# A trunk kernel's first microseconds: the first weights fetched earlier, one half's square sum put after the other half's scaling

## The chip, the core and the metric

The kernel runs on one core of one Trainium2 chip. The metric is the device time of one execution in microseconds (us). The core has a matrix engine (PE; its weight loads are listed as PEld), a vector engine (DVE), a scalar engine (ACT), a general engine (POOL) and a queue engine that only issues transfers (SP). Each engine takes its instructions in the order in which the program lists them.

## What is computed

Two layers of a causal decoder trunk over 256 tokens of width 1024, in float32:

```python
for i in range(DEPTH):                        # DEPTH = 2
    hn = rms_norm(x, norm_mix[i])
    mix = even_mixer(hn, ...) if i % 2 == 0 else odd_mixer(hn, ...)
    x = x + mix
    x = x + sqrelu_mlp(rms_norm(x, norm_mlp[i]), mlp_w1[i], mlp_w2[i])
return rms_norm(x, norm_final)
# rms_norm: y = xf * rsqrt(mean(xf * xf, axis=-1) + EPS) * g
```

What matters here is the very first step, `rms_norm(x, norm_mix[0])`, and the first product with the layer's weights.

## The kernel before

**Tiling.** x is held as two tiles of 128 tokens, `X[0]` and `X[1]` (the first and the second half). A half is normed, transposed by PE in blocks of 128x128 against an identity matrix, and stored as a high and a low part (`xTh`, `xTl`), since each float32 product is made of three products of shortened numbers. Weights come as 196 pieces of up to 128x1024 (512 KB); `raw` is a piece as fetched, `whi` and `wlo` are its two parts, written by ACT (line 470, called "high split" here) and DVE (line 473, "low split"). Pieces 0, 1 and 2 (840, 840 and 560 columns) are the weights of the first unit, `vg`: 280 output columns, eight k steps for each half of x, three matmuls a k step. Pieces 0, 1 and 2 carry k steps 0-2, 3-5 and 6-7. Pieces 3 and 4 are the next unit, `k`. Five raw buffers exist, so five pieces may be fetched before the first is split.

**The start.** Line 501 loads `X[0]`, line 502 the norm weight `gB`, line 503 the identity, line 504 starts the generator `loads()` (lines 447 to 454), which asks for one piece after the other, line 505 loads `X[1]`, lines 506 and 507 two tables (`cst`, `prm`). All are issued on SP. In `first_norms` (lines 894 to 919) PE first spreads `gB` over all rows (line 899); then for each half `rstd` (line 534) takes the square sum, half of the columns on ACT (line 543) and half on DVE (line 546), POOL adds them and takes the power -1/2 (lines 555 and 557), DVE scales two blocks of 512 columns (line 911), PE transposes each block (line 593), ACT writes `xTh` (line 515) and DVE writes `xTl` (line 521).

**Who sets the order.** The program's order is not written out by hand. A planner (`Plan`, lines 201 to 313) plays a rough model of the engines while the program is being written: each step has an assumed duration and an urgency (lower goes first), and an engine that falls free takes the most urgent step whose inputs are there in the model. The order in which steps begin in the model is the order of the instructions on the chip; the chip then keeps to it, whatever arrives first in fact. A step sees another engine's result 0.2 us later (`SEEN`), and a generator that waits for another line's event or for a buffer is held up by 0.2 us as well. A transfer lands, in the model, at the time that line 406 gives:

```python
Plan.moved = max(Plan.moved, plan.now + lat) + n / 0.34e6   # lat 1.3 us, n in bytes
plan.at(Plan.moved + 0.5, lambda: plan.fire(ev))
```

The steps of the norm have urgency -4 (first half) and -3 (second half), the splits of the pieces that are needed next -1, most others 0 to 3. After the unit `vg` the planner places the set-up of a bias table (`bias_setup`, a table look-up by PE at line 709), then the unit `k` with its matmuls at lines 530 to 532.

Of the kernel before, what the change touches and what calls it, by code (L numbers as in the profile page):

```python
# [25 lines left out]
PSUM = bass.MemoryType.PSUM  # L26
# [174 lines left out]
class Plan:  # L201
    """Puts the program's steps out in the order in which a rough model of the engines begins them:
    each engine takes the most urgent step whose inputs are there."""
# [17 lines left out]
    def when(self, deps, line, fn):  # L221
        """Calls fn as soon as the line can see all of deps done."""
        deps = [d for d in deps if d is not None]
        left = [sum(d.time is None for d in deps)]

        def go():
            t = max([self.now] + [d.time + (0.0 if d.line in (line, None) else SEEN) for d in deps])
            self.at(t, fn)

        def one():  # L230
            left[0] -= 1
            if not left[0]:
                go()

        if not left[0]:
            go()
        else:
            for d in deps:
                if d.time is None:
                    d.then.append(one)  # L240

    def step(self, choices, deps=(), urgency=1, bank=None):
        """choices: (line, time, emit) of the engines that can do the step."""
        self.count += 1
        s = Step(urgency, self.count, bank)
        for line, dur, emit in choices:
            self.when(deps, line, lambda line=line, dur=dur, emit=emit: self.arrive(line, s, dur, emit))
        return s.done
# [44 lines left out]
    def spawn(self, gen):  # L293
        """Runs gen; each value it yields is the events it waits for."""
        ev = Event()

        def go():
            try:
                w = next(gen)
            except StopIteration:  # L300
                self.fire(ev)
                return
            w = [w] if isinstance(w, Event) else w
            self.when(w, None, go)

        self.at(self.now, go)
        return ev
# [8 lines left out]
class Slots:  # L316
    """Buffers that are handed on; the one who gets it waits for its last use."""
# [22 lines left out]
    def recall(self, item):  # L340
        """Takes an item out as soon as it is free."""
        ev = Event()
        if any(item is i for i in self.items):
            self.items = [i for i in self.items if i is not item]
            self.plan.fire(ev)
        else:
            self.wanted.append((item, ev))
        return ev
# [14 lines left out]
@with_exitstack  # L363
def trunk_kernel(ctx: ExitStack, tc: tile.TileContext, x, w, prm_d, gs, cst_d, eye, out, widths):
# [7 lines left out]
    plan = Plan()  # L372
# [24 lines left out]
    def load(dst, src, deps=(), line=SP, u=0, lat=1.3):  # L397
        """A transfer: issued by an engine, then in turn with the others on the queues."""
        eng = {SP: nc.sync, ACT: nc.scalar, POOL: nc.gpsimd}[line]
        n = int(np.prod(dst.shape)) * 4  # L400
        ev = Event()
        dur = {SP: 0.45, ACT: 0.4, POOL: 1.04}[line]
        issued = plan.step([(line, dur, lambda: eng.dma_start(dst, src))], deps, u)

        def move():
            Plan.moved = max(Plan.moved, plan.now + lat) + n / 0.34e6
            plan.at(Plan.moved + 0.5, lambda: plan.fire(ev))

        plan.when([issued], None, move)
        return ev  # L410
# [4 lines left out]
    def halves(pair):  # L415
        """Room for two pieces in a pair of tiles that are not in use."""
        v = [a.rearrange("p k s -> p (k s)") for a in pair]
        return [(v[0][:, 1024 * i:1024 * i + 1024], v[1][:, 1024 * i:1024 * i + 1024]) for i in range(2)]
# [28 lines left out]
    def loads():  # L447
        for p, n in enumerate(widths):
            got = raws.get()
            yield got  # L450
            r = got.value[:, :n]
            src = bass.AP(tensor=w.tensor, offset=w.offset + int(starts[p]), ap=[[n, 128], [1, n]])
            ev = load(r, src, [got], u=1)
            plan.when([ev], None, lambda p=p, raw=got.value: plan.fire(loaded[p], SP, raw))
# [48 lines left out]
    ident_e = load(ident, eye)  # L503
    plan.spawn(loads())
    x_e.append(load(X[1], x[128:256, :], u=0.5))
# [5 lines left out]
    def split_out(hi, lo, src, n, deps, scale=None, bank=None, u=0):  # L511
        """The high part by ACT, the rest by DVE."""
        def high():
            if scale is None:
                nc.scalar.activation(hi, src, AF.Copy)
            else:
                nc.scalar.activation(hi, src, AF.Copy, scale=scale)

        def low():
            if scale is None:  # L520
                nc.vector.tensor_tensor(lo, src, hi.bitcast(F32), OP.subtract)
            else:
                nc.vector.scalar_tensor_tensor(lo, src, scale, hi.bitcast(F32), op0=OP.mult, op1=OP.subtract)  # L523

        e = act(t_act(n), high, *deps, u=u, bank=bank)
        return [e, dve(t_dve(n), low, e, u=u, bank=bank)]
# [7 lines left out]
    def rstd(t, deps):  # L534
        """(mean(x[t]^2) + eps)^-1/2; ACT squares the left columns and DVE the right ones, starting from the left's
        sum where those come first."""
# [22 lines left out]
    def rvar(t, deps):  # L559
        """1 / (mean(x[t]^2) + eps)."""  # L560
# [6 lines left out]
    def to_xT(t, g, xT, xe, rs, deps, back=()):  # L567
        """Steps that write x[t] * g (* rs) transposed into xT."""
# [78 lines left out]
    def unit_N(src, cuts, n, done):  # L647
        """One bank of columns for each row tile."""
        pcs = [next_piece() for _ in cuts]
        for t in range(2):  # L650
            got = bank_a.get()
            yield got
            prev = got
            for pc, (k0, nk) in zip(pcs, cuts):
                prev = rows_N(src, got.value, t, pc, k0, nk, n, prev)
                if t:
                    pc.release(prev)
            plan.spawn(done(t, got.value, [prev]))
# [3 lines left out]
    def units_N(src, dones):  # L662
        """Two banks of columns for each row tile; part of the second comes before the second tile's first."""
# [16 lines left out]
    def row_mm(bank, src, deps, pc, kt, t, n, prev, first, last, u=1):  # L680
        """bank += rows t of src's column tile kt @ half n of the piece's columns."""
# [57 lines left out]
    begun = []  # L739

    def urgency():
        """Earlier maps go first."""
# [3 lines left out]
    def logits_exp(q, k, par, h, P, sums, b, deps, u):  # L746
        """exp(q.k + bias - max) of one map: [q0 x k0 | q1 x k0 k1], and the row sums."""
# [30 lines left out]
    def turned_P(A, deps, u):  # L778
        """The transposed probabilities, in two parts."""
# [24 lines left out]
    def head_map(q, k, par, h, v, v_e, gate, pair, deps, seen=None):  # L804
        """One causal softmax map of a head; its part of the pair's outputs is added to po."""
# [32 lines left out]
    class Pair:  # L838
        """The outputs of two heads, gathered in one bank."""
# [27 lines left out]
    # ================= layer 0: mixer =================  # L867
# [26 lines left out]
    def first_norms():  # L894
        """g over all rows by the tensor engine; it stays in PSUM for the time."""
# [5 lines left out]

        def first_norm(t):
            rs, e = rstd(t, [x_e[t]])
            yield e
            done = []
            for hf in range(2):
# [6 lines left out]
                plan.spawn(turn_x(t, hf, xT0[0], xT0[1], xs, done[-1], ()))  # L913
            if t == 1:
# [11 lines left out]
    def got_ckv(b, evs):  # L926
        """Both parts of the compression's inputs, the second half-block's tokens below the first's."""
# [14 lines left out]
    def stack_q(dst, ps, b, deps, u=0):  # L942
        """Both parts of q / 8 of a head's rows: one in the head's half, the other in the other half."""
# [11 lines left out]
    def stack_k(hi, lo, ps, b, deps, u=0):  # L955
        """The high part of k twice, and the low part over zeros."""
# [92 lines left out]
    def cmp_hidden(ba, e):  # L1049
        """Compressed keys and values."""  # L1050
# [51 lines left out]
    def cmp_softmax():  # L1102
        """The compressed branch of the eight heads in one."""
# [176 lines left out]
    def add_to_x(bank, slots, dep, t, n, rs=None):  # L1280
        """x[t] += bank (* rs)."""
# [11 lines left out]
    def out_proj(m_e, x_free, nxt):  # L1293
        """x += m @ w; the first tokens go ahead, and their norm runs beside the products of the others.
        Two of the pieces lie in the room of the transposed x."""
# [38 lines left out]
    def mlp(src, x_ready, nxt):  # L1334
        """x += relu(norm(x) @ w1)^2 @ w2, the norm's factor of each token squared at the end."""
# [21 lines left out]
        def turned(t, b, evs):  # L1357
            """Tokens are the rows here: to be turned."""
# [76 lines left out]
    def next_stage(gi, norm):  # L1435
        """The transposed (normed) x of the next stage, one token tile after the other."""
# [19 lines left out]
    def program():  # L1456
# [19 lines left out]
        # layer 1  # L1476
# [44 lines left out]
    def final(t, evs):  # L1521
# [4 lines left out]
        def job():  # L1526
            """x * g waits for the norm's factor."""
# [40 lines left out]
```

## Time and profile before

| | |
|---|---|
| median of 3 runs | 640.43 us (640.12 to 640.68) |
| span of the profiled execution | 638.6 us |
| PE busy | 623.5 us (98% of the span) |
| DVE busy | 402.3 us (63%) |
| ACT busy | 358.8 us (56%) |
| clock granted to PE over the span | 0.996 of full |

The span is counted from the first to the last instruction of the profiled execution; the 1.8 us between it and the median lie around it. The profile has a page with totals and 40 slices of the span, and views that can be asked for a stretch: the timeline (instructions by engine in order of time), the table of waits, the transfers with their time to landing, and a table of busy times by stretch. A PE that is busy 98% of the span leaves little: what matters is where the other 2% lie, and in what order things happen around them.

### The profile page before, as it was taken

How to read it: one execution, taken by the hardware profiler on the slowest of the kernel's cores; microseconds unless marked ns; L12 is line 12 of the kernel's file. 1: busy time of each engine (PE TensorE's matmuls, PEld its weight loads, DVE VectorE, ACT ScalarE, POOL GpSimd, SP SyncE). 2: the span in 40 equal slices, each digit the busy share in tenths (PEclk: the TensorE clock that was granted, in tenths of full speed). 3: DMA queues.
4: the chain of work that ended last, by engine and by line, in shares of the span. 5: the costliest groups of instructions: out<-in, count | busy, mean ns of one | idle time of the engine just before them, and what ended most of it. 6: DMA issues, size and time to landing. Idle time of an engine off the chain costs nothing.

```text
span 638.6 us, 10541 instructions
## 1 busy us (share of the span) xinstructions
PE 623.5 (98%) x4022; PEld 562.5 (88%) x4022; DVE 402.3 (63%) x723; ACT 358.8 (56%) x645; POOL 80.8 (13%) x105
## 2 busy tenths in 40 slices
PE   7999999999999999999999999999999999999995
PEld 5999899778899898999988999978889999898994
DVE  6888698869554545445477688785964454544434
ACT  6777488747645445444444588764764444445421
POOL 2022022210201001011120020110020100101011
PEclk8999999999999999999999999999999999999999
DMA  7995432325765565656527433443576555565501
GB/s 280 320 304 190 141 105 96 131 101 185 256 212 191 179 199 165 204 191 214 183 73 236 155 121 111 132 133 120 173 267 202 195 179 193 176 200 176 165 2 66
DMA packets 33188, 110.49 MB, mean 173 GB/s; under 512 B 3425, under 2 KB 6769, under 8 KB 33138
## 3 DMA queue, kind: packets, MB, share of 16 engines
q1 hardware_dynamic: 32274, 107.21, 51.7%
q0 software_dynamic: 576, 2.10, 0.9%
q8 instruction: 31, 0.51, 0.3%
q10 hardware_dynamic: 288, 0.52, 0.2%
q14 instruction: 19, 0.16, 0.1%
HBM read 107.76 MB, written 1.07 MB: 170 GB/s over the span
## 4 chain that ended last, share of the span: by engine, by line
PE 86%; DVE 6%; ACT 4%; issue 2%; DMA 1%; POOL 1%; SPq 0%; POOLq 0%; DVEq 0%; ACTq 0%
PE ps L531 26%; PE ps L530 26%; PE ps L532 26%; PE ps L756 2%; DVE wlo L473 2%; PE ps L790 1%; DVE KZ L964 1%; PE ps L593 1%; DVE QD L951 1%; ACT KD L961 1%; DMA x<-in_x_dram 1%; ACT QD L947 1%; POOL P L827 1%; ACT KD L960 1%; PE ps L1040 1%
## 5 line engine op out<-in xcount | busy, mean ns | idle before, releaser
L473 DVE TENSOR_TENSOR wlo<-raw,whi 128x1024 fp32r<-128x1024 f32 (+1 forms) x157 | 189.3, 1217 | 74.1 <-ACT whi L470 72.6
L470 ACT ACTIVATE whi<-raw 128x1024 fp32r<-128x1024 f32 (+1 forms) x157 | 163.5, 1052 | 96.8 <-PE ps L532 70.3
L530 PE MATMUL ps<-xTh,whi 128*128 128x256 f32 x592 | 168.9, 285 | 0.0
L531 PE MATMUL ps<-xTl,whi 128*128 128x256 f32 x592 | 166.4, 281 | 0.0
L532 PE MATMUL ps<-xTh,wlo 128*128 128x256 f32 x592 | 166.3, 281 | 0.0
L530 PEld LDWEIGHTS ps<-xTh,whi 128*128 128x128 f32 x592 | 111.7, 189 | 1.1 <-ACT gates L996 0.3
L531 PEld LDWEIGHTS ps<-xTl,whi 128*128 128x128 f32 x592 | 111.7, 189 | 0.7
L532 PEld LDWEIGHTS ps<-xTh,wlo 128*128 128x128 f32 x592 | 111.6, 189 | 0.0
L1348 POOL TENSOR_TENSOR P<-P 128x512 f32<-128x512 f32 x32 | 35.8, 1120 | 320.5 <-ACT P L1345 319.0
L473 DVE TENSOR_TENSOR mTl<-raw,mTh 128x1024 fp32r<-128x1024 f32 x34 | 43.2, 1272 | 23.9 <-ACT mTh L470 23.9
L470 ACT ACTIVATE mTh<-raw 128x1024 fp32r<-128x1024 f32 x34 | 36.0, 1059 | 30.2 <-PE ps L531 20.4
L1345 ACT ACTIVATE P<-ps 128x512 f32<-128x512 f32 x32 | 19.0, 595 | 52.2 <-PE ps L532 52.2
L530 PE MATMUL ps<-whi,Th 128*128 128x512 f32 x120 | 46.9, 391 | 0.0
L532 PE MATMUL ps<-whi,Tl 128*128 128x512 f32 x120 | 46.9, 391 | 0.0
L531 PE MATMUL ps<-wlo,Th 128*128 128x512 f32 x120 | 46.9, 390 | 0.0
L1350 DVE TENSOR_TENSOR Tl<-P,Th 128x512 fp32r<-128x512 f32 x22 | 15.2, 693 | 50.1 <-POOL P L1348 50.1
L770 ACT ACTIVATE P<-P,nm 128x128 f32<-128x128 f32 x80 | 35.5, 447 | 13.5 <-DVE nm L766 13.5
L532 PE MATMUL ps<-xTh,mTl 128*128 128x256 f32 (+1 forms) x128 | 38.1, 297 | 0.7 <-DVE mTl L523 0.7
L530 PE MATMUL ps<-xTh,mTh 128*128 128x256 f32 (+1 forms) x128 | 38.7, 302 | 0.0
L531 PE MATMUL ps<-xTl,mTh 128*128 128x256 f32 (+1 forms) x128 | 38.0, 297 | 0.0
L530 PE MATMUL ps<-whi,xTh 128*128 128x512 f32 (+1 forms) x88 | 34.2, 389 | 0.0
L531 PE MATMUL ps<-wlo,xTh 128*128 128x512 f32 (+1 forms) x88 | 33.3, 378 | 0.2 <-DVE wlo L473 0.2
(219 smaller groups left out, 1193.0 us busy)
## 6 DMA issues: line engine op xcount, KB each, us to landing
raw<-in_w_dram SPq DMA_DIRECT2D x192, 512.0 KB, 4.1
B<-ud SPq DMA_DIRECT2D x1, 2048.0 KB, 11.3
gB<-in_gs_dram POOLq DMA_DIRECT2D x4, 512.0 KB, 4.3
x<-in_x_dram SPq DMA_DIRECT2D x2, 512.0 KB, 4.4
mTl<-kcv SPq DMA_DIRECT2D x4, 240.0 KB, 6.8
raw<-in_w_dram SPq DMA_DIRECT2D x2, 420.0 KB, 6.2
out_dram<-P SPq DMA_DIRECT2D x2, 256.0 KB, 2.0
out_dram<-P ACTq DMA_DIRECT2D x2, 256.0 KB, 2.5
```

The costliest lines, as they stand in the source:

```text
L470: nc.scalar.activation(pc.hi[:, :n], raw[:, :n], AF.Copy)
L473: nc.vector.tensor_tensor(pc.lo[:, :n], raw[:, :n], pc.hi[:, :n].bitcast(F32), OP.subtract)
L530: nc.tensor.matmul(out_, ah, bh, start=start, stop=False)
L531: nc.tensor.matmul(out_, ah, bl, start=False, stop=False)
L532: nc.tensor.matmul(out_, al, bh, start=False, stop=stop)
L593: nc.tensor.transpose(p[:, 128 * k:128 * k + 128], xs[:, 128 * k:128 * k + 128], ident)
L756: nc.tensor.matmul(ps[:, 128 * qt:128 * qt + nk], q[:, par, ts], k[i][:, par, :nk], start=i == 0, stop=i == 1)
L770: nc.scalar.activation(P[:, c], P[:, c], AF.Exp, bias=nm[:, qt:qt + 1], scale=-1.0, accum_out=sums[:, qt:qt + 1])
L790: nc.tensor.transpose(pt[:, c], A[:, c], ident)
L1345: e = act(t_act(512), lambda: nc.scalar.activation(r, b.t, AF.Relu), got, *deps)
L1348: g = pool(1.225, lambda: nc.gpsimd.tensor_tensor(sq, r, r, OP.mult), e)
L1350: h = dve(t_dve(512), lambda: nc.vector.tensor_tensor(hl, sq, hh.bitcast(F32), OP.subtract), f, g)
```

## The change

Three things are changed in the code. The first piece's load gets urgency 0.2 and `loads()` is started ahead of the identity's load, whose urgency becomes 0.4; with `X[1]`'s 0.5 unchanged, SP's order goes from `X[0]`, `gB`, identity, `X[1]`, piece 0, piece 1, ... to `X[0]`, `gB`, piece 0, identity, `X[1]`, piece 1, .... And the second half's norm now begins (both its square sums on ACT and DVE) only when an event `scaled` has fired, which stands for the first half's second scaling; before, it could begin as soon as `X[1]` had landed in the model. The rest of the diff takes out comments.

```diff
-            ev = load(r, src, [got], u=1)
+            ev = load(r, src, [got], u=0.2 if p == 0 else 1)
...
     x_e = [load(X[0], x[0:128, :])]
     g_e = load(gB[0:1, :], gs[0:1, :])
-    ident_e = load(ident, eye)
     plan.spawn(loads())
+    ident_e = load(ident, eye, u=0.4)
     x_e.append(load(X[1], x[128:256, :], u=0.5))
...
+        scaled = Event()
+
         def first_norm(t):
+            if t:
+                yield scaled
             rs, e = rstd(t, [x_e[t]])
             yield e
...
                 plan.spawn(turn_x(t, hf, xT0[0], xT0[1], xs, done[-1], ()))
+            if t == 0:
+                plan.when([done[-1]], None, lambda: plan.fire(scaled, DVE))
             if t == 1:
```

## Rows read from the trace of the kernel before

**Rows 1.** The page: span, PE's busy time, granted clock in 40 slices

```profile
span 638.6 us, 10541 instructions
PE 623.5 (98%) x4022; PEld 562.5 (88%) x4022; DVE 402.3 (63%) x723; ACT 358.8 (56%) x645; POOL 80.8 (13%) x105
PEclk8999999999999999999999999999999999999999
```

**Rows 2.** Waits over the span: who waited for whom, us, times, longest

```profile
PE ps L593 <- DVE P L911: 2.3, 1, 2.3
PE ps L530 <- DVE KZ L964: 1.8, 2, 1.1
PE ps L532 <- DVE mTl L523: 0.7, 1, 0.7
```

**Rows 3.** Timeline, PE and POOL: start, duration, what, idle before and releaser

```profile
4.30 2.25 PE L899 MATMUL ps<-gB,P 1*128 1x512 f32 x4
5.33 0.55 POOL L557 TENSOR_TENSOR rs<-ssq,half 128x1 f32<-128x1 f32 x1
8.84 3.35 PE L593 MATMUL ps<-ident,P 128*128 128x128 f32 x16 [2.29 <-DVE P L911]
11.94 0.37 PE L530 MATMUL ps<-whi,xTh 128*128 128x280 f32 x1
15.09 0.40 PE L531 MATMUL ps<-wlo,xTh 128*128 128x280 f32 x1 [0.16 <-DVE wlo L473]
18.79 0.29 PE L532 MATMUL ps<-whi,xTl 128*128 128x280 f32 x1
19.01 0.52 PE L709 MATMUL ps<-Th,Tl 33*16 33x384 f32 x2
19.46 0.39 PE L530 MATMUL ps<-xTh,whi 128*128 128x256 f32 x1
```

**Rows 4.** Timeline, DVE

```profile
7.42 0.69 DVE L546 CUSTOM_DVE_ANT_0 scr<-x 128x512 f32<-128x512 f32 x1 [2.51 <-DMA x<-in_x_dram]
8.04 2.72 DVE L911 SCALAR_TENSOR_TENSOR P<-x,rs,ps 128x512 f32<-128x512 f32 x4
12.22 1.88 DVE L521 TENSOR_TENSOR xTl<-ps,xTh 128x512 fp32r<-128x512 f32 x3
14.02 3.94 DVE L473 TENSOR_TENSOR wlo<-raw,whi 128x840 fp32r<-128x840 f32 x4
```

**Rows 5.** Timeline, ACT

```profile
7.36 0.63 ACT L543 ACTIVATE scr<-x 128x512 f32<-128x512 f32 x1 [2.43 <-DMA x<-in_x_dram]
8.33 0.90 ACT L470 ACTIVATE whi<-raw 128x840 fp32r<-128x840 f32 x1 [0.25 <-DMA raw<-in_w_dram]
11.28 1.56 ACT L515 ACTIVATE xTh<-ps 128x512 fp32r<-128x512 f32 x3
12.72 2.58 ACT L470 ACTIVATE whi<-raw 128x560 fp32r<-128x560 f32 x3
```

**Rows 6.** Timeline, SP: the issues of X[1] and of pieces 0 to 4

```profile
1.95 0.43 SPq L403 DMA_DIRECT2D x<-in_x_dram  x1
2.41 3.04 SPq L403 DMA_DIRECT2D raw<-in_w_dram  x5
```

**Rows 7.** Transfers X[1], pieces 0 and 1: KB, us from issue to landing

```profile
x<-in_x_dram SPq DMA_DIRECT2D x1, 512.0 KB, 5.3
raw<-in_w_dram SPq DMA_DIRECT2D x1, 420.0 KB, 5.9
raw<-in_w_dram SPq DMA_DIRECT2D x1, 420.0 KB, 6.5
```

**Rows 8.** Stretches: us, busy time of five engines, PE's granted clock, DMA share, GB/s

```profile
9.00:10.00 1.00, 1.00 (x6) 1.00 (x7) 1.00 (x2) 0.24 (x2) 0.09 (x1) 0.50 1.05 425
12.00:13.00 1.00, 0.96 (x8) 0.75 (x7) 1.00 (x3) 1.00 (x3) 0.00 (x0) 1.00 0.94 367
```

**Rows 9.** Timeline, DVE, a low split between attention steps

```profile
112.92 1.21 DVE L473 TENSOR_TENSOR wlo<-raw,whi 128x1024 fp32r<-128x1024 f32 x1
```

## The prediction

> **What bounds the kernel now.** First the page: PE is busy 98% of the span at almost full clock, and only the first of the 40 slices shows a lower clock [rows 1]. So PE's own stream sets the end, and the question is where its few idle microseconds lie. The table of waits says where: one wait of 2.3 us, for the first scaling by DVE, and some small ones later, 1.8 us for the low part of k (KZ) and 0.7 us for an attention output (mTl) among them [rows 2]. Then the timeline of the start. PE spreads the norm weight until 6.55, stands still, and begins to transpose at 8.84 [rows 3]. POOL had the first half's factor at 5.33 + 0.55 = 5.88 [rows 3], but DVE's next instruction was the second half's square sum, which waited for X[1] until 7.42; only behind it, at 8.04, came the scaling of the first half [rows 4]. ACT stood in the same place, for X[1] until 7.36 and then for piece 0 until 8.33 [rows 5]. The first weight matmul is at 11.94, the unit's third k step waits for the low split of piece 1 until 15.09, and the next unit begins at 19.46 [rows 3]; no wait of PE worth a row lies between that and the attention part. What the change is worth is therefore read at one place: when does the unit k begin, instead of 19.46?
>
> **What arrives when.** X[1] is issued at 1.95 and takes 5.3: it lands at 7.3. Piece 0 is issued at 2.41 and takes 5.9: 8.3 [rows 6, 7]. Piece 1, SP's next issue (five take 3.04, so at about 2.9), takes 6.5 and is there at about 9.4 [rows 6, 7]: 420 KB cost 1.1 us in the queue. SP's queue holds the same five transfers up to X[1] and piece 0 in both kernels, and the share of the DMA engines is full there [rows 8]. I take it that the last of the five ends where the last ended: X[1] lands at 8.3 instead of 7.3, and pieces 1 to 4, the tables and all behind them land as before. Piece 0 moves ahead: at best X[0]'s landing (the first square sums begin at about 4.2, as POOL's add before 5.33 allows) plus 1.1, so 5.3; at worst at the pace of X[1], whose 512 KB and the identity's 64 KB took from 4.2 to 7.3, which makes 2.3 us of 420 KB: 6.5. Either way its high split of 0.90 [rows 5] ends by 7.4, when DVE is through with the scaling; the two ends of this bound cost the same. The identity lands a little later, before 7.3, and its first user, the transposition, needs it at 6.7: 0.6 us at the worst, hidden behind the waits below.
>
> **The new order.** The planner's model fixes the order on every engine, and it can be worked by hand from its constants; no time is taken from it. Transfers: X[0] 3.99, piece 0 5.27, identity 5.46, X[1] 7.00, pieces 1 to 4 at 8.27, 9.11, 10.65, 12.20, the last four as before. DVE: first-half scaling 5.99 and 6.66, low split 0 at 7.32, square sum 8.26, xTl of the first half 8.93 and 9.53, then idle at 10.14; low split 1 is ready at 10.246 and the second half's scaling at 10.263, so the split goes first by 0.017; scaling 11.19 and 11.85, low splits 2 and 3 at 12.51 and 13.17, xTl of the second half 14.30 and 14.90, low split 4. ACT: high split 0 at 5.67, xTh 7.69, square sum 8.16, xTh 8.77, high splits 1 to 4 at 9.25, 10.05, 11.05 and 12.60, and only then the second half's xTh, ready at 12.92. The same working for the kernel before gives low split 0 between the first and second xTl, and the square sum (5.74) just ahead of the scaling (5.99), which is what the trace has [rows 4]. So the change does two opposite things: it brings the first half forward, and it sends the second half behind four splits.
>
> **The sum, with durations of the trace.** DVE: scaling at 5.9; the second block waits for the weight's second row, 6.55 [rows 3], and ends at 7.3. Low split 0: the four low splits in rows 4 have 3448 columns and 3.94 us, 1.14 ns a column; 840 columns are 0.96: 8.3. Square sum on X[1] at 8.4, 0.69: 9.1. Two xTl at 1.88 / 3 = 0.63: 10.4 [rows 4]. Low split 1 needs the high split 1, which ACT starts behind its own square sum (8.4 to 9.1) and an xTh of 1.56 / 3 = 0.52, at 9.6, and ends at 10.5 [rows 5]: 11.5. Two scalings at 2.72 / 4 = 0.68: 12.8. Low splits 2 and 3, 0.64 and 1.17: 14.7. The second half's first xTl: 15.3. On ACT the same place is reached earlier: piece 4 lands at about 9.4 + 1.1 x 1304 / 420 = 12.8, its split takes 1024 of the 2608 columns of 2.58 us, 1.0, and xTh ends at 14.3 [rows 5, 7]. PE has done all 24 matmuls of the first half by then (nine from about 9.8, the rest behind low splits 1 and 2 at 11.5 and 13.5), and two of the second half. 22 are left from 15.3; from 15.09 to 18.79 the trace has 28 at 0.132 [rows 3]: 18.2. Before, 29 were left at 15.09. The look-up with two matmuls, 19.01 to 19.46, comes between [rows 3]; its input is on DVE behind low split 4 (second xTl 15.9, split 17.1) and about 0.8 to 1.3 of small steps, 17.9 to 18.4. So the unit k begins between 18.2 + 0.45 = 18.65 and 18.95. I take 18.75, the end nearer to the matmuls' own finish: 0.7 us earlier. What is late next is the second half of x, no longer DVE's wait for X[1].
>
> **What costs nothing.** The added wait is a matter of the program's order: the chip gets no new instruction. SP's issue of X[1] slips by one issue of about 0.5, while the queue still works on X[0]. Behind it the buffers of pieces 0 and 1 come free about 3 us earlier, so pieces 5 and 6 are fetched earlier; they still queue behind the tables, and PE shows no wait for weights after 15.09, so I cost that at nothing; if the cover is gone the price would be one low split, 1.21 [rows 9]. The transposes ran at half clock, granted 0.50 from 9 to 10 and 1.00 again from 12 to 13 [rows 8]: with the 2.29 gap gone that cost falls away as well, but it lies in the first half, which now has room until 15.3.
>
> **The time.** The profiled execution has 638.6 us of span, and 1.8 us lie around it to the median 640.43. PE's stream from 19.46 on has no slack that eats a shift, so 638.6 - 0.7 = 637.9 of span, 639.7 us in all.
>
> **Rivals.** (1) The second half is not late. The order hangs on 0.017 us in the model, and if the scaling goes ahead of low split 1, or the splits do not fill ACT, the gain is up to what the first matmul gains: 11.94 to about 9.8 [rows 3], 2.1 us, 638.3. For it: PE's largest wait is just this one [rows 2]. Against: the working reproduces the order of the kernel before.
> (2) The new offset between PE and the splits makes the planner put later steps in another order. A low split of 1.21 stands between attention steps on DVE [rows 9], where PE waits for KZ and mTl. One wait of 1.1 gone gives 638.6; two more splits ahead of a KZ give 639.7 + 2.4 = 642.1. Nothing in the profile says which sign; that the MLP in between keeps PE covered speaks against much of either.
> (3) Slower by the clock. PE fell to half clock after a gap of 2.29 and kept it for some 3 us of dense work [rows 3, 8]. In the new order PE's work from 8 to 15 is thin: nine matmuls, a wait, some more, a wait. If the clock is still low at 15.3, the 24 matmuls of the second half take 0.264 instead of 0.132, 3.2 us more: 642.9. It decides from about 16 such matmuls, since fewer cost less than the 2.0 us between 639.7 and 641.7. Against it: at half clock the first half's work would fill those gaps. The Trainium skill, TensorE: Matmul & The Clock Gate, section HAM oscillation, says that waits for data between bursts of matmuls make each next burst start cold; by that rule the time is this rival's, and the trace agrees as far as the one gap before 8.84 goes.
> (4) The change does nothing that counts: X[1] lands 0.7 later than I take it, or the look-up is late by as much. 640.4.
>
> **Chances.** Forecast 0.50, its own range 639.2 to 640.4; rival 1 0.20; rival 2 0.10 on either side; rival 3 0.06; rival 4 0.04. A measurement of this kernel can tell about 0.2%, 1.3 us, from no change. Faster by more than that: rival 1, the good half of rival 2 and a low edge of the forecast, 0.20 + 0.10 + 0.04 = 0.34. Slower: 0.10 + 0.06 = 0.16. Same: 0.50. The range 638.2 to 641.8 leaves out the slow ends of rivals 2 and 3 and a little below.
>
> **What the new profile would show.** Right: X[1] used at 8.3 to 8.5, the first scaling at about 5.9, ACT with four high splits between the first and second half's xTh, the second half's xTl at about 14.7, the unit k at 18.6 to 19.0. Rival 1 shows k near 17.4, rival 2 other waits of PE after 100 us, rival 3 a granted clock of 0.5 beyond 15 us. Wrong above all if X[1] lands much off 8.3 or if the order of low split 1 and the second scaling is the other way round.

## The result and the profile after

The changed kernel takes 645.64 us (median of 4 runs, 644.42 to 647.37), the kernel before 640.55 beside it: the ratio is 1.0075, with a 95% interval of 1.0061 to 1.009. It is 5.1 us slower, where 0.7 us of gain were forecast; the time lies above the range.

The page after, answering to [rows 1]:

```profile
span 644.2 us, 10537 instructions
PE 628.1 (98%) x4022; PEld 564.5 (88%) x4022; DVE 403.0 (63%) x723; ACT 359.2 (56%) x645; POOL 76.7 (12%) x105
```

PE is busy 4.6 us longer and the span is 5.6 us longer, at the same number of matmuls. The totals say no more than that, and they hide something: the idle time is only 1.0 us longer, since one long wait left it and others came. The table of waits (who waits for whom: us in total, times, longest), answering to [rows 2], shows that the wait of 2.3 us for the first scaling is gone, and that others have come:

```profile
PE ps L1272 <- DVE od L1262: 2.0, 2, 1.4
PE ps L530 <- DVE KZ L970: 1.6, 2, 0.9
PE ps L531 <- DVE xTl L473: 0.9, 1, 0.9
DVE P L915 <- PE ps L899: 2.5, 2, 1.6
```

The lines above L899 have kept their numbers; L915 is the old L911, L970 the old L964, and L1272 takes an attention output (od) to PE. The last line is DVE's: the scaling now waits for PE, which is still spreading the norm weight. PE's timeline of the start (start, duration, what, idle before it and releaser), answering to [rows 3]:

```profile
4.30 3.78 PE L899 MATMUL ps<-gB,P 1*128 1x512 f32 x4
9.81 0.60 PE L530 MATMUL ps<-whi,xTh 128*128 128x280 f32 x1
13.81 0.43 PE L531 MATMUL ps<-wlo,xTh 128*128 128x280 f32 x1
14.04 0.43 PE L532 MATMUL ps<-whi,xTl 128*128 128x280 f32 x1
16.62 0.30 PE L530 MATMUL ps<-whi,xTh 128*128 128x280 f32 x1
16.75 0.29 PE L531 MATMUL ps<-wlo,xTh 128*128 128x280 f32 x1
20.19 0.52 PE L709 MATMUL ps<-Th,Tl 33*16 33x384 f32 x2
20.64 0.39 PE L530 MATMUL ps<-xTh,whi 128*128 128x256 f32 x1
```

The norm weight took 3.78 us instead of 2.25. The first weight matmul is at 9.81 instead of 11.94, so the change does bring the weights forward; but the matmuls of 280 columns follow each other at 0.23 us up to 15.6 and at 0.13 us behind it. 280 columns in 0.23 us are 1.2 GHz, the lower of the two levels. The unit k begins at 20.64, 1.2 us later than before. DVE and ACT, answering to [rows 4] and [rows 5]:

```profile
6.50 0.75 DVE L915 SCALAR_TENSOR_TENSOR P<-x,rs,ps 128x512 f32<-128x512 f32 x1 [1.62 <-PE ps L899]
8.12 0.75 DVE L915 SCALAR_TENSOR_TENSOR P<-x,rs,ps 128x512 f32<-128x512 f32 x1 [0.88 <-PE ps L899]
16.00 0.69 DVE L521 TENSOR_TENSOR xTl<-ps,xTh 128x512 fp32r<-128x512 f32 x1 [0.18 <-ACT xTh L515]
10.75 3.35 ACT L470 ACTIVATE whi<-raw 128x840 fp32r<-128x840 f32 x4
15.37 0.60 ACT L515 ACTIVATE xTh<-ps 128x512 fp32r<-128x512 f32 x1 [1.27 <-PE ps L593]
```

The four high splits do stand between the halves on ACT, and yet the second half's xTh then waits 1.27 us for PE's transposes. SP issues X[1] at 2.40, and the view of the transfers gives it 5.7 us, answering to [rows 6, 7]; it lands at 8.1:

```profile
2.40 0.43 SPq L403 DMA_DIRECT2D x<-in_x_dram  x1
x<-in_x_dram SPq DMA_DIRECT2D x1, 512.0 KB, 5.7
```

The stretches (us, then busy time of PE, PEld, DVE, ACT and POOL with their counts, PE's granted clock, DMA share, GB/s), first the second one of [rows 8], then the long stretch behind the start and the one that turns out to matter:

```profile
12.00:13.00 1.00, 1.00 (x6) 1.00 (x6) 1.00 (x2) 1.00 (x2) 0.00 (x0) 1.00 1.04 391
20.00:110.00 90.00, 89.49 (x677) 86.02 (x676) 75.52 (x218) 62.08 (x159) 10.07 (x18) 1.00 0.58 185
110.00:140.00 30.00, 25.64 (x166) 21.54 (x165) 21.96 (x63) 19.13 (x59) 6.05 (x10) 1.00 0.36 113
```

The clock of 1.00 in the first of these rows is not a reading: this trace has no record of the clock before 15.7 us, and the view prints 1.00 where it has none. The spacing of 0.23 us says that the clock was the lower one. The last two stretches of before:

```profile
20.00:110.00 90.00, 90.00 (x689) 87.28 (x688) 75.53 (x218) 64.58 (x162) 14.09 (x18) 1.00 0.59 192
110.00:140.00 30.00, 28.14 (x172) 23.93 (x171) 23.47 (x65) 19.35 (x59) 6.67 (x12) 1.00 0.30 106
```

Between 110 and 140 us, a hundred microseconds behind the edit, PE stands still for 30 - 25.64 = 4.36 us instead of 1.86; between 20 and 110 for 0.51 instead of nothing. To place the loss as a whole I counted PE's matmul columns along the timeline of every profiled execution and read off when the same share of all columns was through. The lag against the kernel before is 1.2 us at 20 us, 2.7 at 110, 5.6 at 140 and 5.6 at 620 us (the difference of the spans is also 5.6). So in this execution the start costs 1.2, the stretch from 20 to 140 some 4.4, and all behind it nothing.

### The profile page after: what moved, and what is told of

Its sections match the earlier page's. It is cut to its first block, busy times and chain, and to the rows that moved or that the text cites. A ratio compares the mean times of both kernels' runs of the same rounds, so it can differ in the third digit from the quotient of the medians.

```text
span 644.2 us, 10537 instructions
## 1 busy us (share of the span) xinstructions
PE 628.1 (98%) x4022; PEld 564.5 (88%) x4022; DVE 403.0 (63%) x723; ACT 359.2 (56%) x645; POOL 76.7 (12%) x105
## 4 chain that ended last, share of the span: by engine, by line
PE 83%; DVE 7%; ACT 3%; DMA 2%; issue 2%; POOL 1%; POOLq 0%; DVEq 0%; ACTq 0%; SPq 0%
PE ps L532 25%; PE ps L531 25%; PE ps L530 25%; DVE wlo L473 2%; DMA B<-ud 2%; PE ps L756 2%; PE ps L790 1%; PE ps L593 1%; DVE KZ L970 1%; DVE QD L957 1%; POOL P L827 1%; ACT P L770 1%; ACT KD L967 1%; ACT QD L953 1%; ACT KD L966 1%
## 5 line engine op out<-in xcount | busy, mean ns | idle before, releaser
L1356 DVE TENSOR_TENSOR Tl<-P,Th 128x512 fp32r<-128x512 f32 x22 | 15.2, 692 | 49.4 <-POOL P L1354 49.4
L532 PE MATMUL ps<-whi,xTl 128*128 128x512 f32 (+1 forms) x88 | 34.0, 387 | 0.4 <-DVE xTl L521 0.4
```

The source lines that it names most:

```text
L532: nc.tensor.matmul(out_, al, bh, start=False, stop=stop)
L1356: h = dve(t_dve(512), lambda: nc.vector.tensor_tensor(hl, sq, hh.bitcast(F32), OP.subtract), f, g)
```

## The experiments

**What differs in the program.** From 20 us on the change has edited nothing, so the instructions there were set side by side. The planner has put them in another order: on PE the two kernels differ up to matmul 2206 of the 4022 in the traces, at 353 us. (The expectations below count equal matmuls in a row as one, so their numbers are smaller.) Behind the first steps all of it goes back to one exchange on SP's queue: a run below that makes this exchange alone has the changed kernel's order from 55 us on. The timelines show the exchange. Before (pieces 12 and 13, then B):

```profile
24.16 1.46 SPq L403 DMA_DIRECT2D raw<-in_w_dram  x2
26.15 0.38 SPq L403 DMA_DIRECT2D B<-ud  x1
```

After (pieces 11 and 12, B, and piece 13 as the first of the four behind it):

```profile
24.12 1.41 SPq L403 DMA_DIRECT2D raw<-in_w_dram  x2
25.83 0.38 SPq L403 DMA_DIRECT2D B<-ud  x1
26.34 8.07 SPq L403 DMA_DIRECT2D raw<-in_w_dram  x4
```

B stands behind piece 13 before and ahead of it after. B is the attention's bias table, 2 MB. In the planner's sums B is issued at 24.37 and piece 13 at 23.92 in the kernel before; in the changed one B comes at 23.39 and piece 13 at 23.86. With B ahead the planner reckons piece 13 and those behind it some 6 us later, and arranges the whole attention for that. Two theories stood against each other from here. *Order*: the arrangement that the planner makes with B ahead costs the time, between 20 and 140 us. *Start*: the first steps cost it, and the rest only carries it on.

**The two parts of the program apart.** The instructions that begin in the planner's first 15 to 16 us are held back and put out in the order of the other kernel; all later ones stay. This edit and those below are shown shortened.

```diff
+        if self.now < CUT:          # c: later order of before, first steps of after
+            self.held.append((key, emit))     # d: the other way round
+        else:
+            self.flush()            # held steps, in the other kernel's order
+            emit()
```

> The first steps (up to low split 3 and the transposed x) stand in the order of the changed kernel, every later instruction in the order of the kernel before. Theory (the loss is in the later order): the unit k begins about 1.3 late, as in the changed kernel, and the rest follows: 641.9, ratio 1.002. Rival (the late start itself makes the attention late, whatever its order): 645.6, ratio 1.008.

> The opposite: the first steps in the order of the kernel before, every later instruction in the order of the changed kernel. Theory (the loss is in the later order): the unit k begins at about 19.4 and the attention loses 4 to 5 all the same: 644.5 to 645.5, ratio 1.007. Rival (the late start): 640.6, ratio 1.000.

The change's first steps with the old later order take 641.71 us (640.54 to 643.14; 1.0018 of before, 1.0008 to 1.0027). The old first steps with the new later order take 648.21 us (647.53 to 649.2; 1.0117, 1.01 to 1.0134). The direction is that of *Order*; the second lies 2.7 us above the range it expected, which comes up again below.

**More warm-up.** Each of the six matmuls that PE runs on zeros at the start is given out twice.

```diff
-        pe(0.43, lambda: nc.tensor.matmul(banks[7].t, zero...), zero_e)
+        pe(0.43, lambda: [nc.tensor.matmul(banks[7].t, zero...) for _ in range(2)], zero_e)
```

> The changed kernel with 12 in place of 6 warm-up matmuls on PE, no other instruction moved. In the changed kernel's profile a matmul of 280 columns took 0.23 until 15 us and 0.13 behind it. If the slow matmul clock is what makes the unit k late, the first weight matmuls now come at 0.13 and k begins at 19.0 to 20.0 instead of 20.7; the time falls by 0.7 to 1.7, to 644.0 to 645.0. If the second half's chain on DVE is what makes it late, k stays at 20.7 and the time at 645.6.

645.42 us (644.87 to 646.73): no change. The norm weight then took 1.98 us, but later (at 6.40), the matmuls still ran at 0.23 us up to 15.9, and the unit k began at 20.93. The run did not bring the pace up in time, so it does not tell whether the pace is what makes the unit k late.

**B's place, moved in the plan alone.** Two edits of planned times: in the changed kernel B 0.6 us later, in the kernel before piece 13 0.7 us later.

```diff
         e = load(ud[:, :383], u[:16, :383], [e])
+        e = plan.after(0.6, [e])              # h: changed kernel
         e = load(B, ...)
...
+            if p == 13:                       # i: kernel before
+                yield plan.after(0.7, [])
             ev = load(r, src, [got], ...)
```

> The changed kernel with one planned time altered: the load of the bias table B is put 0.6 us later in the planner's sums, so that it stands behind weight piece 13 on SP's queue, as in the kernel before. The first steps stay the change's own; from TensorE's 383rd instruction on the order is again that of the kernel before. Theory (the place of B in the plan decides the order of the whole attention, and that costs about 4 of the 5.1 us): 641.7 us, as for the kernel with the change's first steps and the old later order, 641.0 to 642.4. Rival (the loss is in the first steps or spread over small things): 644.5 or more.

> The kernel before with one planned time altered: weight piece 13 is held back 0.7 us in the planner's sums, so that B's load goes ahead of it; nothing of the change is in it. The first 20 us stay those of the kernel before; from TensorE's 336th instruction on the order is that of the changed kernel. Theory: 644.5 to 648.5 us without any of the change. Rival (the change's own steps make the loss): 640.2 to 641.0 us.

The whole change with B behind piece 13 takes 641.09 us (640.34 to 642.21; 1.0005, 0.9995 to 1.0014). The kernel before, with nothing of the change but B ahead, takes 646.57 us (644.89 to 647.32; 1.0083, 1.0063 to 1.0103). The stretch tells the same. Of the changed kernel with B behind:

```profile
110.00:140.00 30.00, 28.12 (x177) 24.13 (x176) 23.37 (x67) 20.16 (x62) 6.69 (x12) 1.00 0.32 106
```

and of the kernel before with B ahead, with its waits of PE there:

```profile
110.00:140.00 30.00, 25.89 (x144) 21.78 (x144) 20.76 (x58) 17.40 (x51) 6.07 (x10) 0.89 0.32 106
PE ps L1276 <- DVE od L1266: 1.5, 1, 1.5
PE ps L535 <- DVE xTl L476: 0.9, 1, 0.9
PE ps L534 <- DVE KZ L974: 0.9, 1, 0.9
```

The standing still (1.88 and 4.11 us) goes with B's place and not with the change, and the waits are those of the changed kernel. *Start* has fallen as the main cause.

**The transfer or the order?** Is it that the pieces really land later behind B, or that the engines' order was arranged for it? All engines keep their order and only SP's issues of B and piece 13 change places.

```diff
         def emit():
+            if tag == "B":                    # j: changed kernel; k: the two tags exchanged
+                put_off.append(lambda: eng.dma_start(dst, src))
+                return
             eng.dma_start(dst, src)
+            if tag == ("w", 13):
+                put_off.pop()()
```

> The changed kernel with every engine's order as it is; only SP gives out B's load behind piece 13 instead of ahead of it, which the planner isn't told. Theory (the order of the engines' instructions costs the time): 645.6 us, 645.0 to 646.5. Rival (the late landing of the weight pieces behind B costs it): 641.5 to 642.5 us.

> The kernel before with every engine's order as it is; only SP gives out B's load ahead of piece 13 instead of behind it, which the planner isn't told. Theory (the order of the engines' instructions costs the time): 640.2 to 641.2 us. Rival (the late landing of the pieces behind B): 643.5 to 646 us.

The changed kernel's order with B behind takes 648.09 us (644.53 to 649.53; 1.0102, 1.0069 to 1.0136), 1.6 above the range of *Order*: nothing is won back, so it is the order. The old order with B ahead takes 641.95 us (641.02 to 645.61; 1.0014, 1.0 to 1.0027). That is nearer to *Order*, above its bound by 0.75, and its profiled execution is the longest of its ten runs, 645.61:

```profile
ACT whi L480 <- DMA raw<-in_w_dram: 6.3, 1, 6.3
PE ps L767 <- DVE nm L777: 3.5, 1, 3.5
```

There a high split waited 6.3 us for a piece behind B, and PE lost 3.5 us at 43 us. Behind that wait the granted clock was at the lower level from 43.5 to 46.9 us, and at 50 us the execution was 5.2 us behind. Three more of the ten runs lie above 643 us; they have no trace. So the lateness that the planner reckoned with does happen, in this execution at least, and an order that trusts to an early piece pays for it then: B ahead is not free in the old order either.

**Each half of the change alone.**

```diff
-            if t:                             # a: only the loads' order
-                yield scaled
...
-            ev = load(r, src, [got], u=0.2 if p == 0 else 1)   # b: only the yield
+            ev = load(r, src, [got], u=1)
```

> Only the other half of the change: the loads in the new order and rank, the square sum of the second half not tied to the scaling. The planner puts B ahead of piece 13 and TensorE's order is that of the changed kernel from its 377th instruction on. Theory (the later order): 644.5 to 647.5 us, as the changed kernel, with the same gaps of 2.2 to 2.5 us more standing still between 110 and 140 us. Rival (the tie of the second half makes the loss): 640 to 641.5 us.

> Only one half of the change: the second half's square sum follows the scaling of the first half, the loads stay in the old order and rank. The planner again puts B ahead of weight piece 13, but fits the pieces differently: TensorE's order differs from that of the kernel before up to its 794th instruction, some 110 us into the run, and is the same from there on, so the order around 110 to 130 us is that of the kernel before. Theory (what costs is the order around 110 to 130 us, where TensorE stands still): 640.0 to 642.0 us, with no new gaps there. Rival (B ahead of piece 13 costs by itself, in whatever order): 644 us or more.

The loads alone: 646.39 us (644.83 to 647.54; 1.0081, 1.0063 to 1.0099), with 30 - 25.95 = 4.05 us of standing still from 110 to 140 us. The second half's wait alone: 643.11 us (642.81 to 643.62; 1.0033, 1.002 to 1.0045). Either half by itself puts B ahead. The second missed both expectations: the stretch from 110 to 140 us is nearly the old one (2.17 us of standing still), but its first steps lag 1.2 us and the stretch from 20 to 110 adds 1.2. Its order on PE also meets the old one later than the expectation says, at 119 us and not at 110 (two transposes at 128 us still differ). It is a third order, with a price between.

**A better start with the old order.** The change's load order, but the second half's transposes ahead of the weight matmuls that follow; everything behind it as before.

```diff
-  ACT: whi0  xTh  square sum  xTh  whi1 whi2 whi3 whi4  xTh xTh
+  ACT: whi0  xTh  square sum  xTh  whi1  xTh xTh  whi2 whi3 whi4
```

> The later order of the kernel before on every engine; only some twenty first instructions are put in another order: the first weight pieces ahead of the second half of x on SP, as in the change, the square sum of the second half behind the first half's scaling, but the second half's transposes ahead of the weight matmuls of the second column block, so that they don't stand behind four splits. Theory (the change's front loses what it gains to TensorE's slow pace up to 13.6 to 15.6 us): 640.0 to 641.5 us, no gain worth the name. Rival (the front as such is worth what the prediction gave it, and only the reordering spoiled it): 639.6 us or less.

641.8 us (640.38 to 642.75; 1.001, 1.0001 to 1.002): no gain, 0.3 above the range expected, though PE begins the weight matmuls 3.9 us earlier than before. PE's rows and a stretch of it:

```profile
8.04 0.40 PE L572 MATMUL ps<-whi,xTh 128*128 128x280 f32 x1
19.64 0.38 PE L572 MATMUL ps<-xTh,whi 128*128 128x256 f32 x1
12.00:13.00 1.00, 1.00 (x8) 1.00 (x6) 0.42 (x1) 0.49 (x1) 0.00 (x0) 0.50 1.06 415
```

It is at the lower level up to 15.2 us, by the spacing of its matmuls, and begins the unit k at 19.64, where the kernel before has 19.46.

**Both kernels once more.**

> The changed kernel once more, for a second profiled execution. If the moment at which TensorE comes to full pace belongs to the execution and not to the kernel: the first weight matmul again at 9.8 us, the matmuls 0.23 us apart again from there, but the change to 0.13 us at another time than 15.6 us, anywhere from 13 to 16; between 110 and 140 us again 4.0 to 4.6 us without a matmul, with or without a slow stretch in the granted clock; 644.4 to 648 us. If it belongs to the kernel: 15.6 us again within 0.2.

> The kernel before once more, for a second profiled execution. If the moment of full pace belongs to the execution: the first weight matmul at 11.9 to 12.3 us, the change to 0.13 us spacing anywhere from 11.9 to 15, and 640 to 642 us with it. If it belongs to the kernel: at 12.3 us again within 0.2, and the gB rows in 2.25 us again.

644.46 and 640.77 us. Of the second execution of the changed kernel:

```profile
4.30 2.28 PE L899 MATMUL ps<-gB,P 1*128 1x512 f32 x4
6.72 1.36 PE L593 MATMUL ps<-ident,P 128*128 128x128 f32 x8
8.07 0.40 PE L530 MATMUL ps<-whi,xTh 128*128 128x280 f32 x1
19.18 0.52 PE L709 MATMUL ps<-Th,Tl 33*16 33x384 f32 x2
19.64 0.38 PE L530 MATMUL ps<-xTh,whi 128*128 128x256 f32 x1
5.91 1.45 DVE L915 SCALAR_TENSOR_TENSOR P<-x,rs,ps 128x512 f32<-128x512 f32 x2 [1.01 <-POOL rs L557]
14.56 0.69 DVE L521 TENSOR_TENSOR xTl<-ps,xTh 128x512 fp32r<-128x512 f32 x1 [0.33 <-ACT xTh L515]
12.00:13.00 1.00, 1.00 (x6) 1.00 (x6) 1.00 (x2) 0.77 (x1) 0.00 (x0) 0.50 1.03 381
```

In the second execution of the kernel before, the norm weight took 3.78 us, with the same row as in the first execution of the changed kernel. So the 3.78 us belong to the execution, not to the kernel: both kernels have them once and 2.25 or 2.28 once. I had expected the first weight matmul at 9.8 again; it came at 8.07. The moment of full pace was 15.2 and 15.7 in the changed kernel, 11.7 and 13.9 in the one before.

The record of the clock in the traces sorts all executions with six warm-up matmuls into two kinds. In four (before, changed kernel again, better start, and the old first steps with the new later order) it rises at 4.8 to 5.0 us, falls at 8.2 to 8.4 and rises again at 11.7 to 15.3; there the norm weight takes 2.2 to 2.3 us. In the other nine the first thing on record is the rise, at 12.4 to 15.7 us, and the norm weight takes 3.8.

**All executions side by side.** Lag of PE's work against the first profiled execution of before, as above, at three times; us:

| kernel | first steps | later order | at 20 | at 140 | at 620 | median |
|---|---|---|---|---|---|---|
| before, again | before | before | 0.3 | 0.4 | 0.4 | 640.77 |
| after's first steps only | after | before | 0.5 | 0.5 | 0.5 | 641.71 |
| after, B later in plan | after | before's from 66 us on | 1.0 | 1.3 | 1.4 | 641.09 |
| better start | own | before | 0.2 | 0.3 | 0.4 | 641.8 |
| before, SP's issues exchanged | before | before | -0.1 | 5.2 | 5.2 | 641.95 |
| after | after | after | 1.2 | 5.6 | 5.6 | 645.64 |
| after, again | after | after | 0.2 | 4.2 | 4.1 | 644.46 |
| more warm-up | after | after | 1.5 | 5.5 | 5.4 | 645.42 |
| loads alone | own | after's from 64 us on | 0.6 | 7.2 | 7.2 | 646.39 |
| before, piece 13 later in plan | before | after's from 55 us on | -0.2 | 6.4 | 6.4 | 646.57 |
| after, SP's issues exchanged | after | after | 0.5 | 7.8 | 7.9 | 648.09 |
| after's later order only | before | after | 1.9 | 8.9 | 8.8 | 648.21 |
| second half's wait alone | own | third | 1.2 | 2.9 | 2.9 | 643.11 |

With the old order and B behind, the lag grows by 0.3 at most from 20 to 140 us; with the new one by 4.0 to 7.4, whatever the first steps are. The old order with B ahead is the exception, with 5.3 in the one execution traced, its slowest of ten: all of it comes at 43 us, by the late piece, and not at the end of the attention. Of the new order, the lower growths (4.0 to 4.5) are those where the granted clock stays 1.00 between 110 and 140 us, the higher ones (6.5 to 7.4) those where it is 0.89 there: in four of seven executions PE falls to the lower level for a part of that stretch, at the last of the waits (from 125.0 to 131.8 us in the kernel before with B ahead in the plan). This is where the 648 of the second experiment comes from, in the execution traced.

## Why the prediction was wrong

**The step that failed** is "What costs nothing" together with "PE's stream from 19.46 on has no slack that eats a shift": I followed the planner's sums by hand up to 15 us and costed all behind that at nothing. The mechanism stood there as rival 2, put down to splits that move between attention steps, with 0.10 on its slow side and at most 2.4 us. Its mechanism is what the trace shows; its size is 4.0 to 4.5 us where the clock holds and 6.5 to 7.4 where it falls. PE's waits at the end of the attention in the changed kernel:

```profile
119.46 0.53 PE L1272 MATMUL ps<-ident,od 128*128 128x128 f32 x2 [1.44 <-DVE od L1262]
125.27 0.50 PE L531 MATMUL ps<-xTl,mTh 128*128 128x512 f32 x1 [0.87 <-DVE xTl L473]
126.86 0.50 PE L530 MATMUL ps<-whi,mTh 128*128 128x512 f32 x1 [0.86 <-DVE KZ L970]
116.90 1.21 DVE L473 TENSOR_TENSOR wlo<-raw,whi 128x1024 fp32r<-128x1024 f32 x1
116.92 1.24 POOL L1260 TENSOR_SCALAR dm<-dm 128x2 f32<-128x2 f32 x1
119.11 0.48 DVE L1262 TENSOR_SCALAR od<-od,dr 128x128 f32<-128x128 f32 x2 [0.61 <-POOL dr L1261]
124.01 2.34 DVE L473 TENSOR_TENSOR xTl<-raw,xTh 128x1024 fp32r<-128x1024 f32 x2
126.38 0.43 DVE L970 TENSOR_TENSOR KZ<-ps,KD 64x256 fp32r<-64x256 f32 x1
```

DVE does two splits at 124.01 and only behind them the last KZ, at 126.38, for which PE waits until 126.86. The longest wait, for od, comes from the split at 116.90, but not by DVE's order alone: POOL's step on the way to od (L1260) runs beside that split and takes 1.24 us, and DVE, back from the split, waits 0.61 us more for POOL. In the kernel before no split runs beside this step and it takes 0.19, and the two splits of xTl come behind both KZ:

```profile
115.42 0.19 POOL L1254 TENSOR_SCALAR dm<-dm 128x2 f32<-128x2 f32 x1 [2.57 <-ACT osq L1252]
120.93 0.86 DVE L964 TENSOR_TENSOR KZ<-ps,KD 64x256 fp32r<-64x256 f32 x2
121.81 2.36 DVE L473 TENSOR_TENSOR xTl<-raw,xTh 128x1024 fp32r<-128x1024 f32 x2
```

That is "two more splits ahead of a KZ", as rival 2 has it; the longer step on POOL is a part that it has not. Without the split there the step would be 1.05 us shorter, which I estimate to be worth about 1.0 of the 1.44 us. What I missed is the lever. I looked for a small shift between PE and the splits; it was a large transfer that changed places with a weight piece at 24 us, because the two stood 0.45 us apart in the plan and the change moved them against each other by 0.9. The prediction's reason against it, that the MLP covers PE, was beside the point: the loss is made before the MLP, which neither adds to it nor gives it back. Of the 4.0 to 4.5 us, PE's standing still explains 2.8 (0.31 + 2.48, second execution) to 3.0 (0.51 + 2.50). The rest, 1.2 to 1.4 us, is matmuls that follow each other more slowly, most of it between 20 and 110 us, and I have not taken it apart. Of the two signs that the prediction names for being wrong above all, neither came: X[1] and the order at the start are as forecast. What came was rival 2's sign, other waits of PE after 100 us.

**The gain at the start** failed too, by less: 0.7 us earlier was forecast, 0.2 and 1.2 us later were measured for the unit k. Point by point:

- *The order of the engines* up to the second half came out as derived, low split 1 ahead of the second scaling by its 0.017 us included. *X[1]* landed at 8.1 (forecast 8.3).
- *The first scaling* began at 5.91 in the second execution (forecast 5.9), with the first weight matmul at 8.07 and the second half's xTl at 14.56 (forecast 14.7). In the first execution it waited for the norm weight until 6.50 and 8.12. I had taken the 2.25 us of [rows 3] for a fixed time. Only by this delay did the first execution have its first weight matmul at 9.81, near the prediction's 9.8: that is luck.
- *The half clock.* The prediction put the fall of the clock down to the gap of 2.29 us and let its cost fall away with the gap. In the second execution of the changed kernel PE has no such gap, its transposes (6.72) following the norm weight (until 6.58), and the clock falls all the same, at 8.4 us; it rises at 15.2, where the first execution of the kernel before has 11.7.
- *The matmuls left.* The sum had 22 of the second half left at 15.3. In the second execution the full pace begins at 15.2, and from 15.35 to the look-up at 19.18 there are 29: 29 x 0.132 = 3.8, where 22 make 2.9. These seven are the whole difference between 18.75 and 19.64. The sentence that failed is the one against rival 3, "at half clock the first half's work would fill those gaps": it filled them, and at 0.23 us a matmul it ran on until the second half was there. So rival 3 was right that the clock takes the gain of the start. It was wrong in its price: the second half itself ran at full pace, and 0.9 to 1.9 us are lost against the forecast instead of 3.2.
- *Rival 1* (second half not late) has fallen: the better start removes the lateness and still has the unit k at 19.64. *Rival 4* (nothing) describes what the first steps are worth by themselves: 640.4 there, 641.09 to 641.8 measured with the old order.

The rule weighed in the prediction (the Trainium skill, TensorE: Matmul & The Clock Gate, section HAM oscillation: bursts between waits start cold) is borne out between 110 and 140 us in four of seven executions of the new order, with a granted clock of 0.89 over the stretch, and not in the other three, with 1.00 and nearly the same waits.

What stays open: what sets the moments at which the clock rises and falls in an execution, and whether an order exists that beats both kernels. None of those tried does.

## What to carry to other kernels

Where a planner or a list scheduler writes the order, an edit's price is not where the edit is. Follow its queues in the plan until the two orders have met again, and look first at near ties that involve a large transfer: here 0.45 us between a 2 MB table and a weight piece cost 4 us and more, the edit itself some 1.2 us at the start. To see whether a loss lies in the edit or in the reordering, put the old order behind the new first steps and the new order behind the old ones: two runs settle it. And before the first microseconds are shortened by starting PE's work earlier, look at the pace at which that work will run: three starts with the first weight matmul at 8.0, 9.8 and 11.9 us reached the next unit within 1.2 us of each other.

## What the runs showed of the hardware

A granted clock of 1.00 at the start of a trace need not be a reading. The first execution of the changed kernel has no record of the clock before 15.7 us, and the views print 1.00 there: so from 12 to 13 us, with matmuls of 280 columns 0.23 us apart. The second execution has a record, and its row says 0.50 from 12 to 13 us at the same 0.23; the record's rise at 15.2 is where the spacing goes to 0.13. So where the record is missing, the spacing of equal matmuls tells the level.

And PE held the lower level for long under nearly unbroken work: in the kernel with the better start from 8.4 to 15.2 us, with a single pause of 0.61 us; in the kernel before, which pauses 2.29 or 0.86 us ahead of its transposes, full pace came at 11.7 and 13.9 us.

A small step of POOL took 1.24 us beside a low split of DVE (116.92 to 118.16 us, the split from 116.90 to 118.11) in the changed kernel, and 0.19 without one in the kernel before. All seven executions of the new order have the 1.24. What makes it long, the runs don't show.
